# Places of large tiles in SBUF: positions in steps of 64 bytes, a queue of weight places, shared raw places

## The chip, the cores and the metric

One core of a Trainium2 chip runs the whole program once. The metric is the device time of that one execution in microseconds (us), taken as the median of several executions. All data is float32.

## What is computed

Two model blocks, one after the other, on 256 tokens of width 1024 (T = 256, D = 1024). The first block has a state-space mixer, a gated feed-forward layer (FFN) with a short convolution, an attention without softmax, and a second such FFN. The second block has two layers of: a SwiGLU FFN, a hybrid mixer (sliding-window attention, a gated delta rule, two branch products and an output product), another SwiGLU FFN, each with a LayerNorm after it. Cut to what matters here:

```python
def swiglu(x, w13, w2):
    gate, up = jnp.split(x @ w13, 2, axis=-1)      # w13: 1024 x 5632
    return (jax.nn.silu(gate) * up) @ w2           # w2: 2816 x 1024
# hybrid mixer, its dense parts:
hcat = x @ w_in
return (gate_a * (ya @ w_branch_a) + gate_b * (o @ w_branch_b)) @ w_out
```

Nearly all the work is products of 256 tokens with large weight matrices, which are read once from HBM.

## The kernel before, in words

**Three products for one.** A float32 operand is kept as two float32r tiles, a high part h (the value as ScalarE's copy rounds it) and a low part l (the value minus h, by VectorE); that is `split`, lines 148 to 156. A product is then h·l + h·h + l·h, three float32r matmuls (`mm3`, line 179). In a matmul one operand is *loaded* as weights (128 columns, its own LDWEIGHTS instruction, written PEld in the profile) and the other one is *moved* through the array, 256 or 512 columns at a time. In the profile a matmul's names are out<-moving,loaded: `ps<-xx,wh` moves the activations xx past a loaded piece of wh.

**Weight units.** A weight matrix comes in units of 128 x 1024 numbers (512 KB). `unit` (line 158) takes a raw place, has SP's DMA queue fill it (line 161), takes a place for the split (a pair wh, wl, lines 166 and 167) and splits. ScalarE writes wh, VectorE writes wl. A raw place is free again after the split, a pair after its last matmul.

**Places.** There are 3 raw places (`WR`) and 4 pairs in one rotating pool `wp` (`WP` - 1). In all stages but the hybrid mixer and the short stretches between stages there is a fifth pair in a pool `spare` (line 133); a counter `turn` (line 164) sends every fifth unit there. Units that are loaded ahead for the next stage (`stay=True`, from `ahead`, line 244) never use the spare pair, since it is given up at the end of the stage. Units of the last rows of a stage's row product (`hold=True`) go to pairs of their own (`hold_pools`, line 138); they may have raw places of their own too. That is so in the gated product after the state-space mixer (`c.hold_pools(ctx, 4, 2)`, line 907) and in the output product of the hybrid mixer (`MH, MR = 5, 2`, lines 497 and 1648): there 5 of the 8 units of w_out are held, and their DMAs go through 2 raw places `hraw`.

**The four shapes of products.**
- *column product* (`cols_steps`, line 199): per 128 rows k of the weight three matmuls of 256 columns each, xx moved, wh, wh, wl loaded. Hybrid mixer and attention.
- *wide product* (`wide_steps`, line 207): per k a 512-column matmul (high and low part of xx together, wh loaded) and a 256-column one (wl loaded). The up and gate products of all FFNs.
- *row product* (`rows`, line 192): 512 columns of w moved, an activation loaded (g, the gated activations, in the FFNs; xx in the output products).
- *token product* (`toks`, line 229): 256 columns of w moved, xx loaded; the units loaded ahead, z and v.

**Order of the work.** TensorE runs in the order in which the program is written (`manual_schedule`, line 1599); `weave` (line 65) merges chains of dependent small steps with the dense products as filling. The other engines and the DMA queues are ordered by the program's scheduler from a model of the time line. At the end of each stage the held units are multiplied for the first half of the tokens, then for the second (`last_rows`, line 276), with the normalisation of the first half running meanwhile; the loads ahead for the next stage are asked for just before.

**Where the tiles lie.** Pools lie one behind the other in each partition, in the order in which they are opened, every tile rounded up to 32 bytes. The small tile `mhalf` (line 106, 4 bytes, so 32) lies in front of all others but the identity. So everything behind it starts at an odd multiple of 32 bytes. Positions within 256 bytes that follow from this:

| tile | position | 
|---|---|
| xx (both activation pairs), all k, high and low part | 160 |
| raw, and the 4 pairs wh, wl | 160 |
| spare and held pairs wh, wl in the FFNs | 224 |
| g, high and low part (gh, gl) | 224 |
| keep (the delta rule's result, moved in the last branch product) | 96 |
| spare pair in the state-space mixer, used by one unit | 128 |

All of these except the last are 32 above a multiple of 64. Since rows of xx and pieces of a unit are whole multiples of 256 bytes apart, a product runs at one and the same distance between the moved and the loaded tile from its first k to its last.

Of the kernel before, what the change touches and what calls it, by code (L numbers as in the profile page):

```python
# [9 lines left out]
F32 = mybir.dt.float32  # L10
F32R = mybir.dt.float32r
# [4 lines left out]
P = 128  # L16
T = 256
D = 1024
KD = D // P
FF = 2816  # L20
MF = FF // P
ALPHA = 4.0 ** 0.25
EPS = 1e-6
LN_EPS = 1e-5


# [64 lines left out]
class Core:  # L91


    def __init__(self, ctx, tc, I, O):
        self.tc, self.nc, self.I, self.O = tc, tc.nc, I, O
        self.drams = 0
        self.const = self.pool(ctx, "const", 1)
        self.hp = [self.pool(ctx, "h0", 1)]
        self.tiny = self.pool(ctx, "tiny", 8)
        self.psum = self.pool(ctx, "psum", 8, space=PSUM)  # L100
        nc = self.nc
        self.pe, self.done, self.tails, self.aside = Tensor(nc.tensor), set(), [], iter(())
        self.early, self.norm, self.spare, self.turn = None, [], None, 0
        self.ident = self.const.tile([P, P], F32, name="ident")
        nc.sync.dma_start(out=self.ident, in_=I["ident"])
        self.mhalf = self.const.tile([P, 1], F32, name="mhalf")
        nc.vector.memset(self.mhalf, -0.5)

    def dram(self, *sh):
# [18 lines left out]
        return b[:, :n].rearrange(f"p ({' '.join(names)}) -> p {' '.join(names)}", **dict(zip(names, shape)))  # L128

    def weight_pools(self, ctx, raw, parts):  # L130
        self.raw, self.wp = self.pool(ctx, "raw", raw), self.pool(ctx, "wp", parts)

    def spare_pool(self, ctx):

        self.spare = self.pool(ctx, "spare", 1)
        ctx.callback(setattr, self, "spare", None)

    def hold_pools(self, ctx, parts, raw=0):

# [18 lines left out]
    def unit(self, src, share=0, hold=False, stay=False):  # L158

        raw = (self.hold_raw if hold else self.raw).tile([P, 1024], F32, name="raw")  # L160
        self.nc.sync.dma_start(out=raw, in_=src)
        pool = self.hold if hold else self.wp
        if self.spare and not (hold or stay):
            self.turn = (self.turn + 1) % WP
            pool = self.wp if self.turn else self.spare
        h = pool.tile([P, 1024], F32R, name="wh")
        l = pool.tile([P, 1024], F32R, name="wl")
        with self.behind_norm():
            self.split(h, l, raw, share)
        return h, l  # L170
# [165 lines left out]

    def pair(self, i):

        both = self.hp[i].tile([P, KD, 2, T], F32R, name="xx")
        return both[:, :, 0], both[:, :, 1], both  # L340

    def ktiles(self, x):
# [85 lines left out]
    def ffn(self, x, state, up, down, gate, tail, after):  # L428

        nc = self.nc
        with ExitStack() as ctx:
            self.hold_pools(ctx, HOLD)
            self.spare_pool(ctx)
            act, once = self.pool(ctx, "act", 4), self.pool(ctx, "once", 1)
            gp = self.pool(ctx, "gp", LAG + 2)
            acc, held, gts = [self.ps() for _ in range(4)], [], {}
            self.done.discard("first")  # L440

            def gated(m, s, u, p):
                nc.vector.tensor_tensor(out=p, in0=s, in1=u, op=ALU.mult)
                gts[m] = tuple(gp.tile([P, T], F32R, name=f"g{i}") for i in "hl")
                self.split(gts[m][0], gts[m][1], p)

            def first():
                yield from self.behind(state, x)
                for c in range(2):
                    u = once.tile([P, 2, T], F32, name=f"u{c}")  # L450
                    nc.scalar.copy(out=u, in_=state[c][0])
                    state[c] = u
                self.done.add("first")

            def turn():
                yield "first"
                yield HOP
                for m in range(2):
                    ps = self.ps(2, T)
                    for c in range(2):  # L460
                        for t in range(2):
                            self.pe.transpose(ps[:, c, t * P:(t + 1) * P], state[c][:, t, m * P:(m + 1) * P], self.ident)
                    gated(m, gate(act, ps[:, 0, :], m), ps[:, 1, :], act.tile([P, T], F32, name="sum"))

            def main():
                for m in range(2, MF + LAG):
                    if m % 4 == 0:
                        next(self.aside, None)
                    if m < MF:
                        for c in range(2):  # L470
                            ps = self.ps(2, T)
                            yield from self.wide_steps(ps, self.unit(up[m - 2, c]), self.ktiles(x))
                            if c == 0:
                                s = gate(act, self.fold(act, ps), m)
                        u = self.fold(act, ps)
                        gated(m, s, u, u)
                    j = m - LAG
                    if j < 0:
                        continue
                    w = self.unit(down[j], hold=j >= MF - HOLD)  # L480
                    if j < MF - HOLD:
                        for t in range(2):
                            self.rows(acc, w, t, gts[j], j == 0, False)
                            yield 1
                        del gts[j]
                    else:
                        held.append((w, gts[j], False))
                yield from self.last_rows(acc, held, tail)

            weave(self, [[turn()]], [first(), main()] + after, drain=True)  # L490
# [3 lines left out]
TAIL = 3.9  # L494
LAG = 7
HOLD = 6
MH, MR = 5, 2
TS = 8
NC = T // TS
NG, GC, NP = 64, 16, 64  # L500
# [549 lines left out]
WR, WP = 3, 5  # L1050
# [510 lines left out]
def mixer_inputs(c, pool):  # L1561

    nc, I = c.nc, c.I

    def const(name, *sh, part=P):
        t = pool.tile([part, *sh], F32, name=name)
        nc.gpsimd.dma_start(out=t, in_=I[name])  # L1570
        return t

    c.mixer_consts = (const("sel", NHH, NHH), const("cut", T, part=NHH), const("masks", 2, P),
                      const("levels", 2, CH), const("blocks", 4, 16))
    with ExitStack() as ctx:
        one = c.pool(ctx, "rb", 1)
        rb = one.tile([32, 16], F32, name="rb")
        nc.gpsimd.dma_start(out=rb, in_=I["rel_bias_2"])
        hot = one.tile([32, 3 * P], F32, name="hot")
        nc.gpsimd.dma_start(out=hot, in_=I["buckets"])  # L1580
        neg = one.tile([16, 3 * P], F32, name="neg")
        nc.gpsimd.dma_start(out=neg, in_=I["band"])
        yield
        ps = c.ps(3 * P)
        c.pe.matmul(ps[:16], lhsT=rb, rhs=hot, start=True, stop=True)
        nc.vector.tensor_tensor(out=neg, in0=neg, in1=ps[:16], op=ALU.add)
        ext = c.dram(16, 3 * P)
        c.d_bias = c.dram(16, P, 3 * P)
        nc.gpsimd.dma_start(out=ext, in_=neg)
        for h in range(0, 16, 4):  # L1590
            nc.gpsimd.dma_start(out=c.d_bias[h:h + 4], in_=ext[h:h + 4, None, :].to_broadcast([4, P, 3 * P]))
# [3 lines left out]
def build(ctx, tc, I, O, stages):  # L1595
    c = Core(ctx, tc, I, O)
    nc = tc.nc
# [42 lines left out]
    for n, (_, kind, i, j) in enumerate(plan):  # L1640
        if kind == "mix":
            cT = hybrid(c, i, hT, state, 1 - place)
        else:
            place = 1 - place
        with ExitStack() as cn:
            if kind == "mix":
                c.spare_pool(cn)
                c.hold_pools(cn, MH, MR)
            c.norm_pools(cn)
            g, b = c.gains(I["ln_g_2"][i, j]), c.gains(I["ln_b_2"][i, j])  # L1650
            nc.gpsimd.tensor_scalar(out=x, in0=x, scalar1=ALPHA, scalar2=0.0, op0=ALU.mult, op1=ALU.add)
            ho = c.pair(place)
            next_state, go = ahead(n + 1, ho)

            def tail(t, acc):
                if t == 0:
                    c.done -= {"in0", "in1"}
                c.ln(t, acc, 0.5, g, b)
                if n + 1 == len(plan):
                    nc.sync.dma_start(out=O["out"][t * P:(t + 1) * P], in_=x[:, t])  # L1660
                    return
                yield from c.arrive(ho, x[:, t, :], t)

            if kind == "mix":
                weave(c, [], [c.row_gemm(I["w_out_2"][i], c.ktiles(cT), tail, MH), go], drain=True)
            else:
                c.ffn(hT, state, I["ffn_w13_2"][i, j // 2], I["ffn_w2_2"][i, j // 2], c.silu_gate, tail, [go])
        hT, state = ho, next_state
# [220 lines left out]
```

## Time and profile before

| | us |
|---|---|
| median of 3 runs | 2226.42 (2223.49 to 2230.21) |
| the profiled execution's own time | 2223.28 |
| its span (first to last instruction) | 2221.5 |
| TensorE busy | 2135.0 (96%) |
| VectorE busy | 1537.0 (69%) |
| ScalarE busy | 1182.5 (53%) |
| GpSimd busy | 226.9 (10%) |
| SP's DMA queue, share of 16 engines' span | 50.4% |

How to read it: busy time of a matmul includes the time in which it drains, and matmuls overlap, so what a matmul costs in a dense stretch is not its duration but the distance from its start to the start of the next one. The time line prints starts, and merges neighbours of one kind into one line with a count, so this distance is read from it by subtracting starts. At TensorE's full clock of 2.4 GHz, 256 columns at one column a cycle are 106.7 ns.

### The profile page before, as it was taken

The numbers are of one execution on the slowest core, as the hardware profiler recorded it, in microseconds if no ns is written. First come the engines' busy times: TensorE is split into PE (matmuls) and PEld (weight loads), VectorE is DVE, ScalarE is ACT, GpSimd is POOL, SyncE is SP. The second block draws the span as 40 slices with busy tenths as digits, with TensorE's granted clock in tenths as the row PEclk, the third lists the DMA queues.
The fourth block names the chain that finished last, engine by engine and source line by source line (L and its number), as shares of the span: only waits on it lengthen the run. The fifth ranks groups of instructions, "written<-read, shape, count | busy, mean of one in ns | idle before, by whom it ended". The sixth has DMA issues, their size and how long they took to land.

```text
span 2221.5 us, 36550 instructions
## 1 busy us (share of the span) xinstructions
PE 2135.0 (96%) x13908; PEld 1867.4 (84%) x13908; DVE 1537.0 (69%) x2615; ACT 1182.5 (53%) x2187; POOL 226.9 (10%) x360
## 2 busy tenths in 40 slices
PE   8889999999999999998999899999999899998998
PEld 7677888898888888897889788888889788997886
DVE  8855767576877666787755676676678876576665
ACT  4644656444655555465655355545546555544553
POOL 1001000000000000243400000000005242000000
PEclk9889999999999999999999999999999999999999
DMA  4325576543666565554434545555655453264663
GB/s 143 101 35 175 182 247 198 163 124 125 199 189 203 177 189 188 170 173 147 131 105 134 208 152 189 189 191 189 190 171 169 137 167 111 95 206 153 190 190 123
DMA packets 123471, 362.02 MB, mean 163 GB/s; under 512 B 24732, under 2 KB 38000, under 8 KB 123296
## 3 DMA queue, kind: packets, MB, share of 16 engines
q1 hardware_dynamic: 117696, 350.25, 50.4%
q0 software_dynamic: 5232, 9.37, 1.5%
q8 instruction: 110, 1.80, 0.3%
q14 instruction: 65, 0.53, 0.1%
q10 hardware_dynamic: 368, 0.07, 0.0%
HBM read 355.36 MB, written 5.04 MB: 162 GB/s over the span
## 4 chain that ended last, share of the span: by engine, by line
PE 74%; DVE 8%; DMA 7%; issue 4%; ACT 3%; POOL 1%; POOLq 0%; SPq 0%; DVEq 0%; ACTq 0%
PE ps L36 71%; PE ps L40 3%; DVE wl L154 3%; ACT wh L150 2%; DMA raw<-in_w_out_dram 2%; DMA raw<-in_ffn_w_dram 1%; DMA raw<-in_ffn_w_down_dram 1%; DMA raw<-in_w_in_z_dram 1%; DMA raw<-in_ssm_w_glu_dram 1%; DVE keep L1075 1%; DMA k<-scratch 1%; DVE prod L530 1%; POOL k L1074 0%; DVE k L1075 0%; DMA raw<-in_kv_w_v_dram 0%
## 5 line engine op out<-in xcount | busy, mean ns | idle before, releaser
L36 PE MATMUL ps<-xx,wh 128*128 128x256 f32 (+1 forms) x4064 | 1077.4, 340 | 4.6 <-DVE xx L154 2.6
L154 DVE TENSOR_TENSOR wl<-raw,wh 128x1024 fp32r<-128x1024 f32 (+1 forms) x614 | 738.1, 1204 | 332.5 <-ACT wh L150 322.7
L150 ACT CAST wh<-raw 128x1024 fp32r<-128x1024 f32 x614 | 643.6, 1050 | 324.7 <-PE ps L36 171.0
L36 PE MATMUL ps<-xx,wl 128*128 128x256 f32 x2992 | 803.4, 282 | 0.6 <-DVE wl L154 0.6
L36 PEld LDWEIGHTS ps<-xx,wh 128*128 128x128 f32 x4064 | 686.4, 191 | 91.9 <-issue 18.9
L36 PEld LDWEIGHTS ps<-xx,wl 128*128 128x128 f32 x2992 | 568.4, 190 | 22.0 <-DVE wl L154 0.8
L36 PE MATMUL ps<-wh,xx 128*128 128x256 f32 (+1 forms) x1152 | 258.3, 318 | 0.8 <-DVE xx L154 0.7
L225 ACT COPY sum<-ps 128x256 f32<-128x256 f32 x240 | 88.7, 371 | 251.7 <-PE ps L36 251.6
L36 PE MATMUL ps<-wl,gh 128*128 128x512 f32 x528 | 208.6, 395 | 0.0
L36 PE MATMUL ps<-wh,gl 128*128 128x512 f32 x528 | 207.9, 394 | 0.7 <-DVE gl L154 0.7
L36 PE MATMUL ps<-wl,xx 128*128 128x256 f32 (+1 forms) x576 | 189.7, 329 | 19.3 <-DVE wl L154 18.7
L36 PE MATMUL ps<-wh,gh 128*128 128x512 f32 x528 | 207.5, 393 | 0.0
L36 PEld LDWEIGHTS ps<-wh,xx 128*128 128x128 f32 x1152 | 193.5, 193 | 16.5 <-DVE xx L154 3.0
L226 DVE TENSOR_TENSOR sum<-ps,sum 128x256 f32<-128x256 f32 x240 | 101.2, 423 | 112.1 <-ACT sum L225 112.1
L36 PEld LDWEIGHTS ps<-wl,xx 128*128 128x128 f32 x576 | 111.0, 193 | 31.9 <-DVE wl L154 22.6
L36 PEld LDWEIGHTS ps<-wh,gl 128*128 128x128 f32 x528 | 99.0, 188 | 24.7 <-DVE gl L154 1.6
L36 PEld LDWEIGHTS ps<-wh,gh 128*128 128x128 f32 x528 | 99.2, 188 | 22.6
L36 PEld LDWEIGHTS ps<-wl,gh 128*128 128x128 f32 x528 | 99.2, 188 | 18.9 <-ACT gh L150 0.3
L332 POOL TENSOR_SCALAR v<-mv 128x1 f32<-128x1 f32 x12 | 7.3, 609 | 858.2 <-DVE mv L388 858.2
L150 ACT CAST xx<-ps 128x512 fp32r<-128x512 f32 (+1 forms) x64 | 31.8, 512 | 116.3 <-PE ps L40 115.8
L154 POOL TENSOR_TENSOR wl<-raw,wh 128x512 fp32r<-128x512 f32 x48 | 76.7, 1604 | 70.1 <-ACT wh L150 63.1
L1075 DVE SCALAR_TENSOR_TENSOR k<-ps,cw,k 128x255 f32<-128x255 f32 x144 | 68.5, 475 | 2.2
(291 smaller groups left out, 2315.3 us busy)
## 6 DMA issues: line engine op xcount, KB each, us to landing
raw<-in_ffn_w_dram SPq DMA_DIRECT2D x264, 512.0 KB, 3.6
raw<-in_ffn_w_up_dram SPq DMA_DIRECT2D x88, 512.0 KB, 4.2
raw<-in_w_in_qkv_dram SPq DMA_DIRECT2D x48, 512.0 KB, 4.0
raw<-in_ffn_w_down_dram SPq DMA_DIRECT2D x44, 512.0 KB, 3.9
raw<-in_w_in_gate_dram SPq DMA_DIRECT2D x32, 512.0 KB, 3.5
raw<-in_w_branch_dram SPq DMA_DIRECT2D x32, 512.0 KB, 3.5
raw<-in_ssm_w_glu_dram SPq DMA_DIRECT2D x16, 512.0 KB, 3.5
raw<-in_w_in_z_dram SPq DMA_DIRECT2D x16, 512.0 KB, 3.8
```

Of the source, the lines that this page charges most:

```text
L36: self.pe.matmul(out, lhsT=lhsT, rhs=rhs, start=start, stop=stop)
L40: self.pe.transpose(out, in_, ident)
L150: o = [self.nc.scalar.copy(out=h, in_=src).ins]
L154: r = e.tensor_tensor(out=l[..., c], in0=src[..., c], in1=h.bitcast(F32)[..., c], op=ALU.subtract)
L225: self.nc.scalar.copy(out=s, in_=ps[:, 1])
L226: self.nc.vector.tensor_tensor(out=s, in0=ps[:, 0], in1=s, op=ALU.add)
L332: nc.gpsimd.tensor_scalar(out=v, in0=ms, scalar1=scale, scalar2=eps, op0=ALU.mult, op1=ALU.add)
L530: e.tensor_tensor(out=o, in0=a, in1=b, op=op)
L1075: stt = lambda o, a, s, b, op0, op1, e=V: e.scalar_tensor_tensor(out=o, in0=a, scalar=s, in1=b, op0=op0, op1=op1)
```

## The change

1. `mhalf` takes 128 bytes, so that the tiles behind it start at multiples of 64: xx, raw and the first pair start at 0 within 256.
2. wh and wl of every place, the tiles g, and each of the 8 slabs of xx are 64 bytes longer (`PAD` = 16 numbers). Slab k of xx then lies at 64·k within 256; the places' wh lie alternately at 0 and 128, their wl at 64 and 192; the g tiles follow each other in steps of 64.
3. The four pairs become four pools with one pair each, in a list; a unit takes the first pair of the list and puts it last. The spare pair is put at the head of the list when it is opened, and is passed over by units that stay.
4. The held units of w_out have no raw places of their own any more, but use the 3 common ones.
5. `neg`, a small table of the window attention, is loaded into the tile of another one (`hot`) after the matmul that reads `hot`.

```diff
-        self.mhalf = self.const.tile([P, 1], F32, name="mhalf")
+        self.mhalf = self.const.tile([P, 1], F32, name="mhalf", padded_shape=[P, 32])
...
-        self.raw, self.wp = self.pool(ctx, "raw", raw), self.pool(ctx, "wp", parts)
+        self.raw = self.pool(ctx, "raw", raw)
+        self.places = [self.pool(ctx, f"wp{n}", 1) for n in range(parts)]
...
         self.spare = self.pool(ctx, "spare", 1)
-        ctx.callback(setattr, self, "spare", None)
+        self.places.insert(0, self.spare)
+        ctx.callback(self.places.remove, self.spare)
...
-        pool = self.hold if hold else self.wp
-        if self.spare and not (hold or stay):
-            self.turn = (self.turn + 1) % WP
-            pool = self.wp if self.turn else self.spare
-        h = pool.tile([P, 1024], F32R, name="wh")
-        l = pool.tile([P, 1024], F32R, name="wl")
+        if hold:
+            pool = self.hold
+        else:
+            pool = next(p for p in self.places if not (stay and p is self.spare))
+            self.places.remove(pool)
+            self.places.append(pool)
+        h = pool.tile([P, 1024], F32R, name="wh", padded_shape=[P, 1024 + PAD])
+        l = pool.tile([P, 1024], F32R, name="wl", padded_shape=[P, 1024 + PAD])
...
-        both = self.hp[i].tile([P, KD, 2, T], F32R, name="xx")
+        both = self.hp[i].tile([P, KD, 2 * T + PAD], F32R, name="xx")[:, :, :2 * T]
+        both = both.rearrange("p k (a t) -> p k a t", a=2)
...
-                gts[m] = tuple(gp.tile([P, T], F32R, name=f"g{i}") for i in "hl")
+                gts[m] = tuple(gp.tile([P, T], F32R, name=f"g{i}", padded_shape=[P, T + PAD]) for i in "hl")
...
-MH, MR = 5, 2
+MH = 5
...
-        neg = one.tile([16, 3 * P], F32, name="neg")
-        nc.gpsimd.dma_start(out=neg, in_=I["band"])
         yield
         ps = c.ps(3 * P)
         c.pe.matmul(ps[:16], lhsT=rb, rhs=hot, start=True, stop=True)
+        neg = hot[:16]
+        nc.gpsimd.dma_start(out=neg, in_=I["band"])
...
-                c.hold_pools(cn, MH, MR)
+                c.hold_pools(cn, MH)
```

## Rows read from the trace of the kernel before

**Rows 1.** The page: TensorE's busy time, and shares of the chain that ended last.
```profile
PE 2135.0 (96%) x13908; PEld 1867.4 (84%) x13908; DVE 1537.0 (69%) x2615; ACT 1182.5 (53%) x2187; POOL 226.9 (10%) x360
...
PE 74%; DVE 8%; DMA 7%; issue 4%; ACT 3%; POOL 1%; POOLq 0%; SPq 0%; DVEq 0%; ACTq 0%
```

**Rows 2.** Stretch: length, busy PE, PEld, DVE, ACT, POOL, granted clock, DMA share, GB/s.
```profile
237.00:371.00 134.00, 134.00 (x713) 113.85 (x712) 101.08 (x164) 84.80 (x143) 4.95 (x5) 1.00 0.68 214
```

**Rows 3.** Groups of TensorE by shape: count | busy us, mean ns | idle before.
```profile
L36 PE MATMUL ps<-xx,wl 128*128 128x256 f32 x2992 | 803.4, 282 | 0.6 <-DVE wl L154 0.6
L36 PE MATMUL ps<-xx,wh 128*128 128x512 f32 x1920 | 670.5, 395 | 0.0
L36 PE MATMUL ps<-xx,wh 128*128 128x256 f32 x2144 | 406.9, 290 | 4.6 <-DVE xx L154 2.6 <-DVE k L1075 1.0 <-ACT k L274 0.9
L36 PE MATMUL ps<-wl,gh 128*128 128x512 f32 x528 | 208.6, 395 | 0.0
...
L36 PE MATMUL ps<-wh,xx 128*128 128x256 f32 x832 | 154.0, 284 | 0.8 <-DVE xx L154 0.7
...
L36 PE MATMUL ps<-wh,xx 128*128 128x512 f32 x320 | 104.4, 409 | 0.0
```

**Rows 4.** Time line of TensorE, column products, xx then keep moved: start, length, what.
```profile
1226.51 0.40 PE L36 MATMUL ps<-xx,wh 128*128 128x256 f32 x2
...
1226.87 0.40 PE L36 MATMUL ps<-keep,wh 128*128 128x256 f32 x2
...
1227.23 0.39 PE L36 MATMUL ps<-keep,wh 128*128 128x256 f32 x2
...
1227.91 0.39 PE L36 MATMUL ps<-keep,wh 128*128 128x256 f32 x2
```

**Rows 5.** The same, wide product of an FFN: pair at 160, then spare pair at 224.
```profile
250.40 0.40 PE L36 MATMUL ps<-xx,wh 128*128 128x512 f32 x1
...
251.46 0.40 PE L36 MATMUL ps<-xx,wh 128*128 128x512 f32 x1
...
253.22 0.40 PE L36 MATMUL ps<-xx,wh 128*128 128x512 f32 x1
...
253.92 0.40 PE L36 MATMUL ps<-xx,wh 128*128 128x512 f32 x1
```

**Rows 6.** The same, row product of an FFN: w at 160, then held w at 224.
```profile
387.39 0.39 PE L36 MATMUL ps<-wl,gh 128*128 128x512 f32 x1
...
389.49 0.39 PE L36 MATMUL ps<-wl,gh 128*128 128x512 f32 x1
...
398.87 0.39 PE L36 MATMUL ps<-wl,gh 128*128 128x512 f32 x1
...
400.91 0.39 PE L36 MATMUL ps<-wl,gh 128*128 128x512 f32 x1
```

**Rows 7.** The same, row product with w moved from the pair at 128.
```profile
172.75 0.40 PE L36 MATMUL ps<-wl,xx 128*128 128x512 f32 x1
...
173.45 0.40 PE L36 MATMUL ps<-wl,xx 128*128 128x512 f32 x1
```

**Rows 8.** The same, matmuls of plain float32 in the state-space mixer.
```profile
55.30 3.70 PE L36 MATMUL ps<-hT,raw 128*128 128x256 f32 x16
```

**Rows 9.** Time line of TensorE in the first output product: [idle before <- releaser].
```profile
1262.88 0.79 PE L36 MATMUL ps<-wl,xx 128*128 128x512 f32 x1 [4.43 <-DVE wl L154]
...
1268.69 0.80 PE L36 MATMUL ps<-wl,xx 128*128 128x512 f32 x1 [2.87 <-DVE wl L154]
```

**Rows 10.** The chain of waits in the first output product: start, length, what.
```profile
1253.47 1.24 DVE wl L154
1254.72 5.78 DMA raw<-in_w_out_dram
1262.86 3.45 DMA raw<-in_w_out_dram
```

**Rows 11.** TensorE's waits over the whole span: us in total, times, longest.
```profile
PE ps L36 <- DVE wl L154: 19.4, 6, 4.4
```

**Rows 12.** Stretches of the first output product, columns as in rows 2.
```profile
1262.00:1268.00 6.00, 2.93 (x6) 1.66 (x6) 2.65 (x3) 1.90 (x2) 0.00 (x0) 0.50 0.55 186
...
1270.00:1272.00 2.00, 2.00 (x6) 1.56 (x6) 1.39 (x2) 0.00 (x0) 0.00 (x0) 0.57 0.69 285
```

More of the change, by code (lines that the diff above doesn't have):

```diff
@@ L23 @@
 EPS = 1e-6
+PAD = 16
 LN_EPS = 1e-5
@@ L102, in __init__ @@
         self.pe, self.done, self.tails, self.aside = Tensor(nc.tensor), set(), [], iter(())
-        self.early, self.norm, self.spare, self.turn = None, [], None, 0
+        self.early, self.norm, self.spare = None, [], None
         self.ident = self.const.tile([P, P], F32, name="ident")
         nc.sync.dma_start(out=self.ident, in_=I["ident"])
-        self.mhalf = self.const.tile([P, 1], F32, name="mhalf")
+        self.mhalf = self.const.tile([P, 1], F32, name="mhalf", padded_shape=[P, 32])
         nc.vector.memset(self.mhalf, -0.5)
```

## The prediction

> **What bounds the kernel now.** First the page: TensorE is busy 96% of the span, and 74% of the chain that ended last are its instructions; DMA has 7% and VectorE 8% [rows 1]. Then the stretches: in the dense loop of an FFN TensorE is busy for all of its 134 us at the full clock, VectorE for 101 and ScalarE for 85, at 214 GB/s [rows 2]. There the only thing that can shorten the time is fewer or faster matmuls. So the question is what a matmul costs from start to start, and that I read from the time line.
>
> A column product takes 0.36 us for three matmuls of 256 columns, 120 ns each, while xx is moved; 0.3 us later, with keep moved in xx's place, the same three take 0.34 us, 113.3 ns each (1227.23 to 1227.91 holds six) [rows 4]. Shape, weights, place of the weights and the splits beside them are the same. What differs is where the moved tile lies: xx at 160 within 256 bytes like the loaded wh, keep at 96. So **the position of the two tiles that TensorE reads at once has a price**. It is no simple rule. In row products w at 160 with g at 224 takes 2.10 us for nine matmuls, 116.7 ns for 256 columns, and the held w at 224 with g at 224 takes 2.04 us, 113.3 [rows 6]: here the equal position is the fast one, in rows 4 the slow one. The wide product takes 353 ns for its 768 columns with both tiles at 160 (three pairs in 1.06 us), and 350 with the weights at 224 (two in 0.70) [rows 5]: 117 to 118 for 256 columns, hardly different.
>
> Against this the Trainium skill, page "TensorE: Matmul & The Clock Gate", section "Step-by-step: what each phase is for", says that TensorE has two independent read ports, and that loading the next weights takes no read bandwidth from the running matmul. By that rule no position could matter; rows 4 and 6 disagree by 6%, so I don't take it for the sum and keep it as a rival.
>
> **Part by part: positions.** Counts from the groups by shape [rows 3], prices from the time lines [rows 4 to 7], in units of 256 columns:
> - Column: 2144 matmuls load wh, half as many wl, 3216 units at 120 ns: 386 us.
> - Wide: 1920 pairs at 352 ns: 676 us (5760 units).
> - Row products of the FFNs: 528 in each of three groups, one shown; 6 of 22 units are held, so 432 at 226.7 and 1152 at 233.3 ns: 367 us (3168 units).
> - Token: 832, and half as many that move wl, 1248 units; both tiles lie at 160, so I take the column's 120: 150 us.
> - Row products with xx loaded: 320 and half as many, 480 at some 230 ns, between the two prices of rows 6: 110 us (960 units).
>
> That is 14,352 units in 1689 us, 117.7 ns on average. At 113.3, the best price that a row shows, they would take 1627 us: **62 us are paid for position**. With the change the eight slabs of xx step through 0, 64, 128 and 192 while the weight piece stays, so each product meets each of the four distances twice; the g tiles step in the same way. Two of the four distances occur in the rows, the equal one and 64, and each is fast in one shape and slow in another; the other two are in no row. The bounds are none of the 62 us and all of it. I take half, 31 us, since the price should be a mix of both values when every product passes through all distances. Of this some nine tenths should reach the end, as dense loops have TensorE at 134 of 134 us but the hybrid mixer's chains of small steps have not: **28 us**.
>
> VectorE and ScalarE are off the path in the dense loops [rows 2], so a change of their own price by position costs or brings nothing there; if TensorE is 3% faster, the loop of rows 2 takes 130 us and VectorE's 101 still fit. The padding adds no instruction and no DMA.
>
> **Shared raw places.** The output product waits twice for a split, 4.43 and 2.87 us [rows 9]. The chain shows why: two hraw places, each freed by a split, then a DMA of 5.78 us, and once more 3.45 us [rows 10]. The second layer repeats it; four of the six waits for wl in rows 11 are these. TensorE's idleness lowers its clock: it is granted 0.50 of full speed, 1.2 GHz, after the first wait, and is back only near 1272 [rows 12]; the 12 matmuls of these two stretches, each some 0.2 us longer at half the clock, cost 2.4 us. So at most 9.7 us lie here per layer, 19 in all. With three raw places for all eight units the last held one needs one refill less behind the wait for the hold places (whose memory the mixer's tiles free last), so it should come some 5 us sooner; but the loads ahead for the FFN now queue behind the held units, and a held unit blocks a common place until its hold place is free. Bounds: nothing, or a few us lost at the start of the FFN, to 19 us gained. I take **10 us**, two layers by 5. What is late next is the split of the seventh and eighth unit, still behind a DMA.
>
> **List of places.** Same number of pairs, but a stage's first unit gets the free spare pair instead of waiting for one that holds weights loaded ahead. All waits of TensorE for wl are 19.4 us [rows 11], 14.6 of which are the output products' (7.3 in the layer of rows 9, taken twice); so at most 5 us. I take 0: in the loops the splits run ahead of TensorE.
>
> **The table neg.** Its load moves behind a matmul on GpSimd's queue, and the five DMAs behind it wait one DMA longer, 3 to 6 us by rows 10. Its first reader is the hybrid mixer, more than a whole FFN later; that covers it. Without this cover it would cost those 6 us once.
>
> **Sum.** 2223.3 us (the profiled execution's own time) - 28 - 10 = 2185. The median of the runs stands 3.1 above the profiled execution, so 2188.
>
> **Rivals.**
> A. *Alignment frees the stream altogether.* All prices above 113.3 and 113.3 itself are more than plain float32 shows: 16 matmuls of 256 columns start 0.22 us apart (3.70 us less the last one's 0.4, by 15), two cycles a column at 2.4 GHz, so some 108 ns for 256 cycles [rows 8]. If the 32-byte offset of every float32r tile costs the rest, 14,352 units at 108 ns take 1550 us, 139 less; at four fifths, as other engines start to bind, 111, and with 10 of the raw places 2105. Against it: the one unit whose w lies at 128, a multiple of 64, still takes 0.70 us for three matmuls of 512 columns, 116.7 for 256 [rows 7]; but there the loaded xx was at 160. The skill's same page, section "Wait — 56ns, not 53.3ns?", has warm matmuls start N/2.4 ns + 2.5 ns apart; its 109.2 for 256 columns would put the units at an estimated 1567 us; no float32r row shows it.
> B. *Position doesn't matter on average.* TensorE's price stays, either by the two-ports rule, with rows 4 and 6 due to something else, or because the mean over four distances equals today's 117.7, or because the tiles don't end up where the diff says. Then only the 10 us are left: 2216, and no change to be measured if half of these fail.
> C. *Slower: stepping spoils settled streams.* A product now keeps one distance, and its starts settle to a constant spacing. If each change of distance from k to k+1 unsettles it, every unit costs the worst price of the rows, 120 ns: 1722 us, 33 more, 30 at the end, less 10: 2246. It decides from a mean of 119 ns on (17 us more, and the raw places' gain is used up and 0.3% lost). For it: the fast row products at 224 lose their one good distance. Against it: 120 is the price of only a third of the units, and no row shows a mixed stream dearer.
>
> **How the numbers follow.** A measurement can tell 0.3%, some 7 us. Forecast, half the price of position: 0.60, with a range of its own from 2151 (all 62 us, nine tenths, and 19) to 2220 (a tenth of it and no raw gain). A: 0.14. B: 0.18, of which 0.10 within 0.3%. C: 0.08. Two of the forecast's 60 parts fall within 0.3% too. Faster 0.80, same 0.12, slower 0.08. The likeliest time is 2188. The range goes up to 2226, taking in B, and down to 2115, some part of A; left out are C and most of A.
>
> **What would show it.** Right: column products at about 116 ns on average and different from k to k; wide pairs below 350; row products of 512 between 227 and 233; no wait over 3 us in the output products. Wrong: unchanged spacing in all shapes (B); spacing at 108 to 110 (A); 120 and more everywhere (C); or shorter spacing but new waits of TensorE for wl in the FFN loops, which would mean that raw places and not TensorE set the pace.

## The result, and the profile after

The changed kernel takes 2201.25 us (median of 4 runs, 2196.38 to 2204.19) against 2228.32 for the kernel before (4 runs): ratio 0.988, interval 0.986 to 0.991, some 27 us less. Of the profiled executions the one after took 2201.57 us with a span of 2199.7, so 21.8 less than the span of before. A second series gave 0.989 (0.987 to 0.991) and a span of 2204.3: one span scatters by several us.

The page of the kernel after, against [rows 1]: the counts of instructions are the same, and VectorE and ScalarE (1182.5 before) are as busy as before, so position has no price for them that shows. TensorE's busy time has fallen by 14 us.

```profile
PE 2120.7 (96%) x13908; PEld 1855.6 (84%) x13908; DVE 1535.2 (70%) x2615; ACT 1181.9 (54%) x2187; POOL 227.4 (10%) x360
...
PE 68%; DVE 11%; DMA 8%; issue 5%; ACT 4%; POOL 2%; SPq 0%; POOLq 0%; ACTq 0%; DVEq 0%
```

Stretches of the kernel after, columns as in [rows 2]: the dense loop of the FFN, then 24 us of nothing but column products with xx, then 21 us with keep moved.

```profile
234.00:368.00 134.00, 134.00 (x716) 113.98 (x715) 101.65 (x165) 84.86 (x144) 5.46 (x6) 1.00 0.68 215
...
924.00:948.00 24.00, 24.00 (x206) 23.88 (x204) 21.35 (x36) 15.49 (x28) 13.84 (x11) 1.00 0.67 213
1218.00:1239.00 21.00, 21.00 (x181) 21.00 (x180) 16.93 (x26) 11.10 (x16) 0.00 (x0) 1.00 0.63 203
```

The two stretches of column products in the kernel before, at the same places of the program:

```profile
933.00:957.00 24.00, 24.00 (x202) 24.00 (x202) 21.61 (x36) 15.15 (x27) 13.11 (x11) 1.00 0.69 215
1228.00:1249.00 21.00, 21.00 (x186) 20.96 (x185) 17.57 (x29) 10.64 (x17) 0.00 (x0) 1.00 0.60 204
```

Only the count of matmuls matters here: the dense loop holds 716 where it held 713, xx 206 for 202, keep 181 for 186. What was slow became a little faster, and what was fast became slower. The time line of TensorE after, columns as in [rows 4 to 6], shows the same:

```profile
1217.15 0.39 PE L37 MATMUL ps<-keep,wh 128*128 128x256 f32 x2
...
1218.56 0.28 PE L37 MATMUL ps<-keep,wh 128*128 128x256 f32 x1
...
247.23 0.39 PE L37 MATMUL ps<-xx,wh 128*128 128x512 f32 x1
...
250.37 0.39 PE L37 MATMUL ps<-xx,wh 128*128 128x512 f32 x1
...
383.73 0.39 PE L37 MATMUL ps<-wl,gh 128*128 128x512 f32 x1
...
385.81 0.39 PE L37 MATMUL ps<-wl,gh 128*128 128x512 f32 x1
...
395.00 0.40 PE L37 MATMUL ps<-wl,gh 128*128 128x512 f32 x1
...
397.10 0.39 PE L37 MATMUL ps<-wl,gh 128*128 128x512 f32 x1
```

Twelve matmuls of keep in 1.41 us are 117.5 ns (113.3 before). Nine wide pairs in 3.14 us are 349 ns (352). Nine row matmuls of 512 columns take 2.08 us from common places (2.10 before) and 2.10 from held ones (2.04 before).

For whole kernels I took the distance from each float32r matmul's start to the next one's, over the whole trace, and left out as waits all above 128 ns (256 columns) or 250 ns (512); matmuls at half the clock fall out with them. The means, with those of the experiments below:

```
ns, start to start            before  after  e3     e5     e6     e8     e11
column, 256 columns (x3216)   119.6   117.5  119.6  114.9  115.2  117.9  116.0
token, 256 (x1248)            119.7   118.0  119.7  117.1  117.2  118.2  117.8
wide pair, 512 + 256 (x1920)  350.3   348.2  350.2  352.5  351.9  349.0  352.4
row with g, 512 (x1583)       231.5   232.3  231.2  228.0  230.9  229.6  227.7
row with xx loaded, 512 (x480)229.6   232.1  229.6  230.1  231.3  231.6  228.0
keep, 256 (x384)              113.4   118.0  113.4  118.7  117.8  118.7  118.7
```

(e2 is as before, e4 as after, to 0.2 ns.) Counts times differences, before to after: column -6.7 us, wide -4.1, token -2.1, row with g +1.3, row with xx +1.2, keep +1.8: **8.6 us less**, not 31.

The waits of TensorE after (us in total, times, longest), against the 19.4 us of [rows 11]:

```profile
PE ps L41 <- DVE x L399: 11.2, 5, 4.2
...
PE ps L37 <- DVE wl L157: 4.3, 4, 2.0
```

The waits for wl in the output products [rows 9] are gone, and the kernel waits for x, the LayerNorm's result, instead. In TensorE's time line (first and second layer):

```profile
1264.11 1.11 PE L41 MATMUL ps<-ident,x 128*128 128x128 f32 x4 [3.94 <-DVE x L399]
...
1999.81 1.11 PE L41 MATMUL ps<-ident,x 128*128 128x128 f32 x4 [4.22 <-DVE x L399]
```

VectorE's time line and the chain of waits in the first output product show why:

```profile
1254.98 0.69 DVE L392 BATCH_NORM_STATS2 st<-xn 128x6 f32<-128x512 f32 x1
1257.36 2.48 DVE L157 TENSOR_TENSOR wl<-raw,wh 128x1024 fp32r<-128x1024 f32 x2 [1.69 <-ACT wh L153]
1259.75 0.69 DVE L391 SCALAR_TENSOR_TENSOR xn<-ps,x 128x512 f32<-128x512 f32 x1
...
1250.25 7.18 DMA raw<-in_ffn_w_dram
...
1258.61 1.23 DVE wl L157
```

Between the LayerNorm's two halves of a row stand two splits of the FFN's units loaded ahead. VectorE waits 1.69 us ahead of the first for ScalarE's wh; the unit of the second came by a DMA of 7.18 us that landed at 1257.43, so that its split could start only at 1258.61, behind ScalarE's.

Where the time went, by stage, from the starts of the same matmul in each trace (us against before; a minus is gained):

```
stage (us in before)     e2     e1     e7     e3     e5     after  again
state-space, 4-214      -0.6   -1.7   -5.3   -8.3   -4.4   -3.0   -5.9
FFN, 214-393             0.0    0.1   -0.2   -0.1   -0.3   -0.8   -0.8
attention, 393-448      -1.7   -1.9   -4.4   -5.4   -1.1   -4.1   -2.7
attention, 448-546       3.3    3.2    1.1   -0.3    0.7    1.2    1.4
three FFN parts, 546-919 -1.0  -0.3   -1.2   -2.6    1.3   -2.8   -1.0
mixer, 919-1252          0.4    1.3    0.6    0.7    0.3    0.5    0.3
output product, -1284    1.2   -4.7    0.9   -3.8   -0.2   -3.7   -5.4
FFNs, 1284-1658          0.8   -0.2   -0.6    2.3    2.2   -2.7    1.1
mixer, 1658-1994         1.6    0.4    1.1    1.9   -0.4   -1.1   -0.4
output product, -2025    1.7   -3.8    0.0   -3.5    0.9   -4.8   -3.3
```

e2 changes nothing that acts, as its experiment shows; its column is what one trace scatters by, up to 3 us a stage. Two things stand out in the column of the kernel after: the output products give 8.5 us, and the hybrid mixers, with most of the column products, 0.6. A third is small but clean: in the FFN at 214 to 393, where TensorE has next to no wait, the stage moves by the sum of its own spacings' differences, to 0.1 us, in twelve traces (after: -0.8, by its spacings -0.8; e5: -0.3, by its spacings -0.4; e11: -0.6, by its spacings -0.7).

### The profile page after: what moved, and what is told of

Same layout as the page of the kernel before. It is cut to its first block, busy times and chain, and to the rows that moved or that the text cites. A ratio compares the mean times of both kernels' runs of the same rounds, so it can differ in the third digit from the quotient of the medians.

```text
span 2199.7 us, 36566 instructions
## 1 busy us (share of the span) xinstructions
PE 2120.7 (96%) x13908; PEld 1855.6 (84%) x13908; DVE 1535.2 (70%) x2615; ACT 1181.9 (54%) x2187; POOL 227.4 (10%) x360
## 4 chain that ended last, share of the span: by engine, by line
PE 68%; DVE 11%; DMA 8%; issue 5%; ACT 4%; POOL 2%; SPq 0%; POOLq 0%; ACTq 0%; DVEq 0%
PE ps L37 65%; DVE wl L157 4%; PE ps L41 3%; ACT wh L153 3%; DMA raw<-in_ffn_w_dram 3%; DVE keep L1081 1%; DVE k L1081 1%; DMA raw<-in_w_out_dram 1%; DMA raw<-in_ffn_w_down_dram 1%; DMA k<-scratch 1%; DMA raw<-in_w_in_z_dram 1%; DMA raw<-in_ssm_w_glu_dram 1%; DMA raw<-in_w_in_qkv_dram 1%; DVE prod L536 1%; POOL u L1080 0%
## 5 line engine op out<-in xcount | busy, mean ns | idle before, releaser
L37 PE MATMUL ps<-xx,wh 128*128 128x256 f32 (+1 forms) x4064 | 1065.5, 337 | 4.9 <-DVE xx L157 2.1
L37 PEld LDWEIGHTS ps<-xx,wh 128*128 128x128 f32 x4064 | 678.6, 189 | 91.0 <-issue 18.9
```

Source lines behind the costliest of these rows:

```text
L37: self.pe.matmul(out, lhsT=lhsT, rhs=rhs, start=start, stop=stop)
```

## Experiments

### Is it the multiple of 64 bytes? (e2, e4)

```diff
-        self.mhalf = self.const.tile([P, 1], F32, name="mhalf")
+        self.mhalf = self.const.tile([P, 1], F32, name="mhalf", padded_shape=[P, 32])
```

> The kernel before with mhalf padded to 128 bytes alone: every large tile moves by 96 bytes, to multiples of 64, and all distances between moved and loaded tile stay. Theory 1 (the distance of the two tiles sets the spacing, and the change gains only by mixing distances): column products stay at 119 to 120 ns a matmul, keep at 113 to 114, rows of 512 at 227 (held) and 233; time within 0.3% of before. Theory 2 (the multiple of 64 is what gains): spacing falls in all shapes at once, to 117 to 118 for columns as after the change, 9 us or more faster; in the form of rival A, 108 ns and some 110 us faster.

Measured: ratio 1.0006 (0.999 to 1.002), and every spacing as before. e4 is the other way round, the changed kernel with mhalf unpadded, beside a second series of the changed kernel itself:

> The changed kernel with mhalf back at 32 bytes: all large tiles move by 96 bytes, to 32 above a multiple of 64; the steps of 64 and all else stay. Theory 1 (only the distances count): spacings as after the change, columns 117.5, wide pairs 348, rows with g 232.3 ns, time within 4 us of the changed kernel. Rival (the multiples of 64 count where tiles step): all spacings longer, columns at 119 to 120, 10 us or more slower than the changed kernel.

> The changed kernel once more, on the chip of the three runs beside it, as the measure for them: ratio to before 0.988 to 0.990, spacings as in its first profile.

Measured: 0.991 (0.989 to 0.993) for e4, 0.989 (0.987 to 0.991) for the changed kernel, 2205.9 and 2203.2 us; spacings equal within 0.2 ns. Alignment to 64 bytes does nothing, with a constant distance or in steps; rival A falls.

### Is it the stepping? (e3)

```diff
-PAD = 16
+PAD = 0
```

> The changed kernel with PAD = 0: tiles at multiples of 64, list of places and shared raw places as changed, but no stepping, so the distances are those of before. Theory 1 (stepping mixes the spacings): columns go back from 117.5 to 119.6 ns (3216 of them, 7 us dearer), tokens from 118.0 to 119.7, wide pairs from 348 to 350 (4 us dearer), held rows from 232 to 227 and keep from 118 to 113.4 (4 us cheaper): 8 to 9 us slower than the changed kernel, about 2210, with the wait gains of the output products kept. Theory 2 (alignment, not stepping, made the gain in spacing): as the changed kernel, 2201, columns at 117.5.

Measured: 2211.1 us, ratio 0.994 (0.992 to 0.996); the spacings are back at those of before in every shape, keep and held rows included. So the stepping makes the changed spacings, and the lists and shared places (with neg) make 13 us of the gain by themselves. What stepping adds is 8 to 10 us by the medians and 11 to 13 by the ratios, while the spans of the profiled runs (2202.7 for e3; 2199.7 and 2204.3 with stepping) show 3 us or nothing.

### Does the distance decide? (e5, e6, e11)

e5 puts the weights 64 bytes from xx, and on the position of g:

```diff
     def weight_pools(self, ctx, raw, parts):
+        self.gap(ctx, 16)
...
+    c.gap(ctx, 48)
     c.hp.append(c.pool(ctx, "h1", 1))
```

(`gap(ctx, n)` opens a pool with one tile of n numbers.) e6 moves xx alone, from 160 to 96:

```diff
-        self.mhalf = self.const.tile([P, 1], F32, name="mhalf")
+        self.mhalf = self.const.tile([P, 1], F32, name="mhalf", padded_shape=[P, 56])
...
+        self.gap(ctx, 16)
...
+    c.gap(ctx, 48)
     c.hp.append(c.pool(ctx, "h1", 1))
+    c.gap(ctx, 16)
```

> The kernel before with two gaps alone (64 bytes ahead of the raw places, 192 ahead of the second activation pair): all weight places lie at 224 within 256, xx stays at 160, g at 224. So columns, wides and tokens run at the constant distance 64, all rows with g at the equal position. Theory 1 (the distance decides): columns as keep before, 113.4 in place of 119.6 ns, 20 us; unheld rows as the held ones, 227 in place of 233 for 512, 1152 of them, 7 us; wide pairs 347 to 350 in place of 350.3, 0 to 6 us: 25 to 33 us faster, 2195 to 2203. Theory 3 (the absolute places count, not their distance): columns anywhere from 113 to 120. Theory 4 (position does nothing; keep and held rows were quick for another reason): no change, 2228, columns at 119.6.

> The kernel before with xx alone moved to 96 within 256 (mhalf padded to 224 bytes, and gaps so that every other large tile keeps its position): xx then lies where keep lies, with the weights at 160 as before. Theory 1 and 3 (position, relative or absolute): columns as keep before, 113.4 in place of 119.6 ns: 20 us; tokens, where the two parts are exchanged, between 113 and 120; rows with g unchanged at 227 and 233: some 20 us faster, 2205 to 2210. Theory 4 (position does nothing): 2228, columns at 119.6.

Measured: ratios 0.997 (0.996 to 0.999) and 0.998 (0.997 to 0.999), 4 to 6 us. The spacing moved as theory 1 has it for columns (119.6 to 114.9 and 115.2) and, in e5, rows with g (231.5 to 228.0); wide pairs went the other way (352). Moving the weights (e5) and moving xx (e6) do the same to the columns, and moving both by the same amount does nothing (e2): it is the distance, the moved tile's position less the loaded one's, and not the place of either (theory 3). By counts times differences e5 should have gained 17 us, and gained a third of that. e5's column stretch (columns as above) and its waits for wl:

```profile
929.00:953.00 24.00, 24.00 (x214) 23.87 (x213) 21.72 (x37) 15.84 (x29) 13.75 (x11) 1.00 0.69 218
...
PE ps L36 <- DVE wl L159: 23.8, 11, 5.7
```

214 matmuls in the 24 us that held 202. But in the two hybrid mixers e5's column products take 6.2 and 6.3 us less, and TensorE's waits there (and its slow starts after them) 6.1 and 5.5 us more. In the changed kernel the columns gain 2.8 us in each mixer and the waits grow by 2.8 and 1.2. The trace of the kernel before happens to be quick there: e1, e2, e3 and e7, with its spacings, are 0.4 to 1.9 us longer in each mixer. Against their mean the waits of e5 still grow by some 10 us in all, those of the changed kernel by some 2. **A mixer's column products fill the time beside its chains of small steps; faster filling is followed by waiting.**

One such wait can be followed in e5, a wait for wl of a kind that the kernel before has nowhere in its mixers. TensorE, then VectorE, last VectorE at the same step in the kernel before:

```profile
988.61 0.39 PE L36 MATMUL ps<-xx,wl 128*128 128x256 f32 x1 [1.79 <-DVE wl L159]
...
987.26 0.69 DVE L1079 TENSOR_TENSOR k<-k,masks 128x512 f32<-128x512 f32 x1 [3.49 <-DMA k<-scratch]
987.87 0.68 DVE L159 TENSOR_TENSOR wl<-raw,wh 128x512 fp32r<-128x512 f32 x1
...
990.27 0.75 DVE L1074 TENSOR_TENSOR k<-k,masks 128x512 f32<-128x512 f32 x1 [2.01 <-DMA k<-scratch]
```

The split that TensorE needs stands on VectorE behind a step of the chain, and that step waits 3.49 us for the chain's DMA, 2.01 before. For the other waits only the sums are shown.

The second finding is in e6's traces: its column stretch of 24 us, which goes through all four places of the weights, then the time line of a later one, then keep.

```profile
927.00:951.00 24.00, 24.00 (x213) 23.93 (x212) 21.52 (x36) 15.58 (x29) 13.67 (x11) 1.00 0.70 219
...
976.89 0.39 PE L36 MATMUL ps<-xx,wh 128*128 128x256 f32 x2
...
977.91 0.39 PE L36 MATMUL ps<-xx,wh 128*128 128x256 f32 x2
...
978.25 0.39 PE L36 MATMUL ps<-xx,wh 128*128 128x256 f32 x2
978.61 0.19 PEld L36 LDWEIGHTS ps<-xx,wl 128*128 128x128 f32 x1 [0.17 <-DVE wl L159]
978.62 0.39 PE L36 MATMUL ps<-xx,wl 128*128 128x256 f32 x1
978.84 0.40 PE L36 MATMUL ps<-xx,wh 128*128 128x256 f32 x2
...
979.19 0.40 PE L36 MATMUL ps<-xx,wh 128*128 128x256 f32 x2
...
980.60 0.40 PE L36 MATMUL ps<-xx,wh 128*128 128x256 f32 x2
...
1217.76 0.40 PE L36 MATMUL ps<-keep,wh 128*128 128x256 f32 x2
...
1219.17 0.40 PE L36 MATMUL ps<-keep,wh 128*128 128x256 f32 x2
```

Nine matmuls from 976.89 take 1.02 us, 113.3 ns each. At 978.25 the stream is interrupted (three in 0.59 us, the load of wl waiting for its split), and from then on twelve take 1.41 us, 117.5 ns, though the next unit lies in a place that ran at 113.3 in the stretch of 24 us. **A stream settles to a spacing and keeps it; after an interruption it can settle to the other one.** keep too, at 113.3 before from the same positions within 256 bytes, runs at 117.5 here. Whole traces bear this out. e5's has 178 stretches of twelve column matmuls without a wait: 133 have a mean of 113.3 to 115.2, 45 of 117.5 to 118.2, none lies between, and of 86 that follow another without a wait between them none changes level (in e6, 1 of 84 does). At distance 0, in the kernel before, most lie at 120 and none below 118.

e11 is e8 (below) with the slabs of xx padded by 256 bytes:

> e8_rows_equal with the slabs of xx padded by 256 bytes in place of 64, nothing else: one pair of activations then has only the distances 0 and 256 (within 512) to the weights, by turns from k to k, the other one only 64 and 320. Theory 1 (each distance has its spacing, also when it changes from k to k): columns and tokens of the first pair at 119 to 120 ns, those of the second between keep's 113.4 at 320 and 117.8 at 64, some 115 to 117. Theory 2 (any change from k to k gives the middle): 117 to 118 in both pairs, as e8_rows_equal. Time: within 5 us of e8_rows_equal by either.

Measured: 0.990 (0.988 to 0.993), e8 0.989: no difference in time. Its time line, a column stretch of the first pair, then one of the second:

```profile
1206.83 0.40 PE L37 MATMUL ps<-xx,wh 128*128 128x256 f32 x2
...
1208.27 0.40 PE L37 MATMUL ps<-xx,wh 128*128 128x256 f32 x2
...
1020.46 0.39 PE L37 MATMUL ps<-xx,wh 128*128 128x256 f32 x2
...
1021.82 0.39 PE L37 MATMUL ps<-xx,wh 128*128 128x256 f32 x2
```

Twelve in 1.44 us, 120.0, and in 1.36 us, 113.3; whole-trace means 119.6 (0 and 256) and 115.2 (64 and 320). A change of distance by 256 from k to k disturbs nothing: theory 1. Steps of 64 give 117 to 118 at every distance (column means after the change, by distance: 116.9 to 118.4), so no single distance is read off them.

### A better place for each shape? (e8)

The changed kernel with xx alone in steps:

```diff
-        h = pool.tile([P, 1024], F32R, name="wh", padded_shape=[P, 1024 + PAD])
+        h = pool.tile([P, 1024], F32R, name="wh")
...
+    c.gap(ctx, 48)
     c.hp.append(c.pool(ctx, "h1", 1))
```

(wl and g lose their padding in the same way.)

> The changed kernel with xx alone stepping: the weight places and the g tiles are not padded, and a gap of 192 bytes ahead of the second activation pair puts held and spare places and g where the weights lie (0 within 256). Theory 1 (a constant distance can be better than the mix, per shape): rows with g at 228 in place of 232.3 ns, 1584 of them, 7 us; columns and wides as after the change, 117.5 and 348; so 5 to 7 us faster than the changed kernel in the same kind of run, 2194 to 2197. Theory 2 (stepping is best in every shape, the spacing is a property of the mix): rows stay at 232 and the time at 2201.

Measured: 0.989 (0.987 to 0.991), 2199.2 us. Rows with g are at 229.6 in place of 232.3 (228 expected): 4 us for 1583, of which the wide pairs and columns, 0.8 and 0.4 ns dearer, take back 3. No measurable gain.

### Shared raw places alone (e1)

```diff
-                c.hold_pools(cn, MH, MR)
+                c.hold_pools(cn, MH)
```

> The kernel before with the raw places of the held w_out units shared (no hraw), nothing else. Theory 1 (the shared places alone bring the gain in the output products): the waits of TensorE for wl there, 4.4 and 2.9 us and the same in the second layer, shrink to under 1 us each, a wait of some 4 us for the LayerNorm (ps<-ident,x) comes up behind them in each layer, as it did after the change; net 3 to 6 us a layer, 6 to 11 in all, ratio 0.995 to 0.997; the spacings of all shapes as before. Theory 2 (the list of places is needed too): waits for wl of over 2 us stay and the time is within 3 us of before.

Measured: 0.996 (0.994 to 0.998), 9 us. TensorE's waits in e1, columns as above:

```profile
PE ps L40 <- DVE x L393: 14.0, 5, 5.1
...
PE ps L36 <- DVE wl L154: 2.5, 2, 2.1
```

Both halves of theory 1: 19.4 us of waits for wl became 2.5, none of it in the output products, and the wait for the LayerNorm's x rose from 5.1 to 14.0. By the table of stages 8.5 us are gained in the output products.

### The list of places alone (e7)

The kernel before with item 3 of the change and nothing else.

> The kernel before with the list of places alone (four pools and the spare pair at the head), positions and raw places as before. My step: 0 us, at most 5 faster, and the waits for wl of the output products stay (4.4 and 2.9 us). Rival: the list is what brought the 12 us of waits, then 6 us or more faster. Slower by over 3 us would mean that the counter's fixed turn was better.

Measured: 0.997 (0.995 to 0.999), **7 us faster**, against my 0 and near the rival's figure; but the waits for wl of the output products stay (4.78 and 2.95 us), so the rival's reason isn't it either. The stage that stands out of the scatter is the attention's start, 4.4 us shorter. There, in the 10 us behind its wait for xx, before and in e7:

```profile
432.70:442.70 10.00, 9.96 (x60) 9.49 (x60) 4.34 (x5) 3.98 (x7) 0.00 (x0) 0.69 0.60 192
...
PE ps L36 <- DVE xx L154: 2.6, 1, 2.6
```

```profile
425.50:435.50 10.00, 9.92 (x79) 9.25 (x80) 7.03 (x8) 5.90 (x10) 0.00 (x0) 1.00 0.72 235
...
PE ps L36 <- DVE xx L156: 0.9, 1, 0.9
```

The wait for the split of xx shrank from 2.6 to 0.9 us, and TensorE, granted 0.69 of its clock in the kernel before, has the full clock here: 79 matmuls for 60. The units stand in another order on the queues there, since places come free in another order. How much of this is the list's is not shown: in the two traces of the changed kernel, which has the list, the same wait is 2.1 and 2.3 us, and only one of them keeps the full clock; e2 and e1, without the list, are 1.7 and 1.9 us shorter in this stage too. The other 3 us are in the state-space stage, where e3 and e7 gain most but where e5, without the list, gains 4.4 too; they are not told from scatter.

### The new wait for the LayerNorm (e9, e10)

```diff
-        if self.early:
-            self.early()
-            self.early = None
         for t in range(2):
+            if self.early and t == late:
+                self.early()
+                self.early = None
```

(`late` is true in the hybrid mixer's output product.)

> The changed kernel; in the hybrid mixer's output product the loads ahead for the FFN are asked for after the LayerNorm of the first half has been started, not ahead of the last rows. Theory 1 (the new wait comes from the splits of these units standing in front of the LayerNorm on VectorE): the two waits of some 4 us ahead of ps<-ident,x fall to 2 us or less, 4 to 8 us faster than the changed kernel if the loads are not missed. Rival (the loads ahead are then late): the token products of the FFN's first unit wait for wl by 3 us or more in each layer, and the time is the same or up to 6 us longer.

Measured: 0.989 (0.987 to 0.990), 2197.5 us. The waits ahead of ps<-ident,x fell from 3.94 and 4.22 us to none that the time line shows and 1.02. Theory 1 has the cause. But the token products now wait, 2.2 us a layer, and not for wl as the rival had it. TensorE and VectorE in e9:

```profile
1269.91 0.39 PE L37 MATMUL ps<-wh,xx 128*128 128x256 f32 x1 [2.19 <-DVE xx L157]
...
1264.51 0.74 DVE L399 SCALAR_TENSOR_TENSOR x<-xn,r,gain 128x512 f32<-128x512 f32 x1
1265.17 3.49 DVE L157 TENSOR_TENSOR wl<-raw,wh 128x1024 fp32r<-128x1024 f32 x3
1268.57 0.69 DVE L392 BATCH_NORM_STATS2 st<-xn 128x6 f32<-128x512 f32 x1
1269.18 1.27 DVE L157 TENSOR_TENSOR xx<-ps,xx 128x512 fp32r<-128x512 f32 x2
```

The same splits of wl, 3.49 us, now stand behind the LayerNorm of the first half (its last step is the one at 1264.51) and ahead of the split of xx that the tokens need: the queue of VectorE is moved round, not shortened. e10 joins e8 and a form of e9 in which the first two transfers are asked for early:

```diff
+        if self.early and late:
+            self.first()
```

(`first` issues the two transfers; the split of `unit` follows with the rest.)

> The changed kernel with the two things that helped: weight places and g unpadded and at equal positions (as e8_rows_equal), and in the output product of the hybrid mixer the loads ahead split: the transfers of the first two units are asked for ahead of the last rows, their splits and the other units behind the LayerNorm of the first half. Theory: rows with g at 229 to 230 ns, the waits of 4 us ahead of ps<-ident,x at under 2 us each, and the token products' waits for wl, 2.4 us a layer when all loads came late, gone too: 2.4 + 8 us faster than the changed kernel, some 2190. Rival (raw places run short, or the splits behind the LayerNorm are now late): token products wait for wl by 2 us or more in each layer, 2196 to 2200.

Measured: 0.989 (0.987 to 0.991), 2203.0 us, beside 2203.2 of the changed kernel on the same chip. The token products wait 2.2 us a layer as in e9, again for xx. No version here measurably beats the changed kernel.

## Why the prediction came out as it did

The time came out 13 us above the forecast and inside its range. The direction was right, and one of the three terms had its size. That the whole came so near is in part luck: the largest term came far too short, and the list, put at nothing, brought 7 us when alone.

- **Positions, -28.** This term failed. The spacings gave 8.6 us where 31 were forecast, and of the 5.6 that the mixers' columns gained 4 came back as waits there (some 2 against the four traces with the spacings of before). At the end stepping brought 8 to 13 us (e3), not 28. Two of its choices were wrong. First, "at 113.3, the best price that a row shows": 113.3 is one of two spacings in which a product at distance 64 settles (e6), and keep and the held rows lost theirs when they stepped. I counted what the slow shapes pay, not what the fast ones have to lose: the rows and keep gave back 4.3 of the 12.9 us that columns, tokens and wide pairs gained. I left keep out of the units and took the mean before as 117.7 ns; over the whole trace and with keep it went from 117.2 to 116.6. Second, "nine tenths should reach the end": that holds for the FFN of the stage table, where all of it arrives, but not for columns woven between the mixer's chains (e5: some 12.5 gained, 11.6 given back).
- That position has a price at all was right: xx moved by 64 bytes takes columns from 119.6 to 115.2 ns (e6), and e11 measures 120.0 and 113.3 for the same shape in one execution. The Trainium skill, page "TensorE: Matmul & The Clock Gate", section "Step-by-step: what each phase is for", names two independent read ports and says nothing of where the tiles lie; that position could therefore not matter was my reading of it, and these runs contradict it.
- **Shared raw places, -10.** Right in size: 9 us alone. "What is late next is the split of the seventh and eighth unit" was wrong: it is the LayerNorm, behind splits of the FFN's units on VectorE. I had named those loads as a risk for the start of the FFN, not for VectorE's queue. So the sign "no wait over 3 us in the output products" failed (3.94 and 4.22).
- **List of places, 0.** Wrong: 7 us (3 to 11) alone. I bounded it by TensorE's waits for wl; what changed, as far as one trace shows, is a wait for xx and the clock behind it, which no row of mine held. Alone, the list and the shared places make 7 and 9 us, together with neg 13.
- **neg, and the other engines, 0.** VectorE's and ScalarE's busy times are unchanged. neg wasn't tried alone; no stage behind it stands out.
- **Signs.** Column products at 117.5 in place of 116, and hardly different from k to k (means of 117.0 to 118.6); wide pairs at 348, rows at 232: in their bounds.
- **Rivals.** A falls with e2, and B in its first form with e6. In its second form, a mean equal to today's, B was nearest for TensorE's price, but it left out the list. C falls: no shape went to 119 by stepping, though its words "starts settle to a constant spacing" describe what e6 shows.

Still open: what decides in which of the two spacings a stream settles (in e11 both mixers run their first nine units at 117.8 and the tenth at 114.0, so it is hardly chance), and why wide pairs prefer distance 0 (350.3 against 352.5 ns) where columns prefer 64.

## What to carry to other kernels

Before a faster matmul is counted as time, look at what TensorE does in that stage: in a loop where it is never idle the gain arrives, in products that fill the gaps of other chains much of it can come back as waits. A best case read from one stretch may be a state that the change destroys, so count what the fast shapes lose too. When a wait is taken from an engine, read the queues of the engine that released it: the same instructions then stand in front of the next reader.

## What the runs showed of the hardware that was not expected

- Streams of float32r matmuls keep a steady spacing. Column products: 120.0 ns for 256 columns with both tiles at the same offset within 256 bytes (e11, the kernel before), 113.3 or 117.5 to 118 at a distance of 64 (e5, e6, e11), 118.7 at 128 (keep in e5). Row products are the other way round: 228.0 ns for 512 columns where all lie at the same offset (e5), 231.5 where most are 64 apart (before). An interruption can move a stream of column products at distance 64 from 113.3 to 117.5, 4% for tens of matmuls (e6).
- An offset of 32 or 0 above a multiple of 64 makes no difference (e2, e4: 0.2 ns).
